# RWKV-7, gated delta rule, mLSTM and RG-LRU in one layer: another order of the groups, an output projection in three rounds, and a longer lag for the mixers' matmuls

## The chip, the cores and the metric

One core of one Trainium2 chip. The metric is the device time of one execution in microseconds; the kernel before took 1270.41 us (median of 3 runs, 1268.99 to 1271.3).

## The reference

One decoder layer on a sequence of 256 tokens with 2048 features, all in float32. The input is normalised and multiplied by one wide matrix; its columns feed four recurrent mixers of 512 features each. Their outputs side by side are multiplied by `w_out` and added to the input. A SwiGLU feed-forward part (hidden size 5632) and a last norm follow.

```python
n = rmsnorm(x, attn_norm[l])
u = n @ w_in[l]
u_gdn, u_mlstm, u_rglru, u_rwkv = jnp.split(u, MIXER_SPLITS, axis=-1)
y_gdn = gated_deltanet(u_gdn, ...)    # conv, l2norm, chunked delta rule with a triangular solve
y_mlstm = mlstm(u_mlstm, ...)         # conv, gates, running maximum, chunkwise attention form
y_rglru = rglru_block(u_rglru, ...)   # conv, two small matmuls, gates, linear scan, gelu gate
y_rwkv = rwkv7_time_mix(u_rwkv, ...)  # token shift, small matmuls, scan over chunks, norm, gate
mix = jnp.concatenate([y_gdn, y_mlstm, y_rglru, y_rwkv], axis=-1)
x = x + mix @ w_out[l]
n = rmsnorm(x, ffn_norm[l])
x = x + (jax.nn.silu(n @ ffn_w_gate[l]) * (n @ ffn_w_up[l])) @ ffn_w_down[l]
```

## The kernel before

Every large matrix product is made of three float32r matmuls (`mm3`, L167): both operands are split into a high and a low half, and high x high, high x low and low x high are summed. Weights come as units of 128 x 1024 values. `weights` (L149) loads one unit through SP's queue into one of four `raw` buffers; ScalarE then makes the high half (`whi`) and VectorE the low half (`wlo`), four buffers of each.

The input projection works in groups of 256 columns (`group`, L374). A group is four units with 24 matmuls of 256 columns each, summed in one PSUM bank of the tag `big`. An eviction follows (`shift_mix`, `conv`, `silu2`, `gelu2`), mostly on VectorE and ScalarE.

The mixers are Python generators, two halves of each mixer (`rwkv_half`, `gdn_half`, `mlstm_half`, `rglru_half`), with `gates_mm` and two `joint_solve` besides. `spawn` puts a generator on a list. After each unit `tick(0.65)` adds 0.65 to a counter, and for each whole number every generator on the list runs to its next `yield`, so that a piece of each mixer is written down between two units of the projection; `HOLD` lets a generator pass some ticks. The order in which instructions are written down is their priority, and for each engine the instructions are put into its queue by priority as soon as what they need has been queued. `high_priority(offset=n)` moves instructions n places earlier; weights are moved 20 places ahead (`PRIO`), evictions 40 (`EPRIO`). The mixers' matmuls and transposes go through `Lag` (L401), which places them `LAG` instructions later:

```python
def matmul(self, *a, **k):
    with self.em.tc.high_priority(offset=-LAG):
        return self.em.nc.tensor.matmul(*a, **k)
```

Their results go to four PSUM banks `mx` and one `mxl`. Scratch tiles in SBUF come from lists of slots (`SLOTS`: classes A, B and L of 512 values per partition, class D of 1024) that are handed out first in, first out.

The groups come in the order RWKV, RG-LRU, delta rule, mLSTM. `w_out` (L1183) multiplies the mixers' outputs by the output matrix: a run (L1195) is one quarter (512 columns) of the output and some of the eight mixer halves. Each half in it is one unit of 12 matmuls of 512 columns; a run ends with two additions from PSUM (L1213). Before the first use of a half, `run` ticks until the mixer has finished it and splits it (`split`, L1175). There are two rounds of four runs: first RWKV, RG-LRU and delta rule, then mLSTM. While generators are alive or the groups are under way, banks come from `big` alone (three); later from all eight in turn.

Of the kernel before, what the change touches and what calls it, by code (L numbers as in the profile page):

```python
# [14 lines left out]
D = 2048  # L15
# [6 lines left out]
OFF_GDN, OFF_ML, OFF_RG, OFF_RW = 0, 2056, 4112, 5136  # L22
CDEC = math.exp(-0.5)
TICKS = 0.65
LAG = 20
UNIT = 1024
PRIO = 20
EPRIO = 40
WARM = 14
TAIL = 3  # L30
HOLD = {("rw1", 17): 1, ("gates", 1): 1, ("rg0", 0): 1, ("rg1", 1): 3}
SLOTS = dict(A=12, B=11, L=4, D=16)
NRAW, NHI = 4, 4


RW, RG, GD, ML = OFF_RW, OFF_RG, OFF_GDN, OFF_ML
# [756 lines left out]
def gates_mm(em):  # L793
    nc = em.nc
    gs = em.S()
    ghi, glo = (gs.bitcast(F32R)[:, i * 256 : i * 256 + 256].rearrange("p (k n) -> p k n", k=KT) for i in range(2))
    nc.scalar.activation(ghi, em.gw, AF.Copy)
    nc.vector.tensor_tensor(glo, em.gw, ghi.bitcast(F32), op=ALU.subtract)
    z = em.mx()
    o = z[0:16, 0:T]  # L800
    for k in range(KT):
        em.mm3(o, ghi[:, k, :], glo[:, k, :], em.nhi[:, k, :], em.nlo[:, k, :], start=k == 0, stop=k == KT - 1)
    em.free(gs)
    g = em.S(2)
    gp = em.gp
    U, V = g[0:16, 0:T], g[0:16, T : 2 * T]
    N, B = g[0:16, 2 * T : 3 * T], g[0:16, 3 * T : 4 * T]
    nc.scalar.activation(U, o, AF.Identity, bias=gp[:, 0:1])
    nc.scalar.activation(gp[:, 1:2], gp[:, 1:2], AF.Exp)
    nc.scalar.activation(B, U, AF.Tanh, scale=0.5)  # L810
    nc.vector.tensor_scalar(B, B, 0.5, 0.5, op0=ALU.mult, op1=ALU.add)
    nc.scalar.activation(N, U, AF.Abs)
    nc.scalar.activation(N, N, AF.Exp, scale=-1.0)
    nc.vector.tensor_scalar(V, U, gp[:, 2:3], 0.0, op0=ALU.mult, op1=ALU.max)
    yield
    nc.scalar.activation(N, N, AF.Ln, bias=em.c_one[0:16])
    nc.vector.tensor_tensor(V, V, N, op=ALU.add)
    nc.vector.tensor_scalar(V, V, gp[:, 1:2], None, op0=ALU.mult)
    nc.vector.tensor_tensor_scan(N, em.rs16, V, 0.0, op0=ALU.mult, op1=ALU.add)
    em.free(em.gw_)  # L820
    em.ncd = em.dp.tile([4, T], F32, name="ncd", tag="ncd")
    nc.sync.dma_start(em.ncd, N[0:4, :])
    t = em.mx()
    for i, r in enumerate((U, N, B)):
        for a in range(2):
            em.pe.transpose(t[:, (i * 2 + a) * 16 : (i * 2 + a) * 16 + 16], r[:, a * P : a * P + P], em.ident[0:16, 0:16])
    GT = em.const([P, 3, 2, 16], "GT")
    nc.vector.tensor_copy(GT.rearrange("p i a n -> p (i a n)"), t[:, 0:96])
    em.free(g)
    em.ncs = GT[:, 1]  # L830
    em.nbeta = em.const([P, 2, 4], "nbeta")
    nc.vector.tensor_scalar(em.nbeta, GT[:, 2, :, 4:8], -1.0, None, op0=ALU.mult)
    em.beta = GT[:, 2, :, 4:8]
    em.neg = em.const([P, 4], "neg")
    nc.scalar.activation(em.neg, GT[:, 1, 1, 0:4], AF.Exp, scale=-1.0)
    nc.vector.tensor_scalar(em.neg, em.neg, -1.0, None, op0=ALU.mult)
    yield

    em.c = em.const([P, 2, 4], "ccol")
    nc.vector.tensor_tensor(em.c, GT[:, 0, :, 8:12], GT[:, 1, :, 12:16], op=ALU.add)  # L840
    t = em.mx()
    for a in range(2):
        em.pe.transpose(t[0:4, a * P : a * P + P], em.c[:, a, :], em.ident)
    M = em.S()
    nc.vector.tensor_copy(M[0:4, T : 2 * T], t[0:4, 0:T])
    nc.vector.tensor_tensor_scan(M[0:4, 0:T], M[0:4, T : 2 * T], M[0:4, T : 2 * T], 0.0, op0=ALU.max, op1=ALU.max)
    em.Md = em.dp.tile([4, T], F32, name="Md", tag="Md")
    nc.sync.dma_start(em.Md, M[0:4, 0:T])
    t = em.mx()
    for a in range(2):  # L850
        em.pe.transpose(t[:, a * 4 : a * 4 + 4], M[0:4, a * P : a * P + P], em.ident[0:4, 0:4])
    em.free(M)
    em.M = em.const([P, 2, 4], "Mcol")
    nc.vector.tensor_copy(em.M.rearrange("p a n -> p (a n)"), t[:, 0:8])
    em.enm = em.const([P, 2, 4], "enm")
    nc.vector.tensor_tensor(em.enm, GT[:, 1, :, 12:16], em.M, op=ALU.subtract)
    nc.vector.tensor_scalar(em.enm, em.enm, 80.0, None, op0=ALU.min)
    nc.scalar.activation(em.enm, em.enm, AF.Exp)
    em.mix["gates"] = 1
# [9 lines left out]
def gdn_half(em, hf, Q, K, V, SZ):  # L869
    nc = em.nc  # L870
    KQ = em.S(2)
    KQv = KQ.rearrange("p (s n) -> p s n", s=2)
    for s, X, bias in ((1, Q, em.c_lnq), (0, K, 0.0)):
        silu2(em, X)
        sq = em.S()
        nc.scalar.activation(sq, X, AF.Square)
        z = yield from sums(em, em.onesr, sq)
        rsqrt_ln(em, sq, z, em.c_4eps, ebias=bias)
        nc.vector.tensor_tensor(KQv[:, s, :], X, sq, op=ALU.mult)
        em.free(sq, X)  # L880
        yield
    silu2(em, V)
    z = em.mx()
# [25 lines left out]
    for g in range(2):  # L909
        z = em.mx()  # L910
# [8 lines left out]
    z = em.mx()  # L919
# [9 lines left out]
    for b in range(4):  # L929
        r = slice(32 * b, 32 * b + 32)  # L930
# [7 lines left out]
    X, XT = em.S(c="B"), em.S(c="B")  # L938
# [104 lines left out]
def mlstm_half(em, hf, Q, K, V1, SO, v1s):  # L1043
# [3 lines left out]
    while "gates" not in em.mix:  # L1047
        yield
    zb = bcast_rows(em, em.Md, hf)
    yield  # L1050
    Hs = em.S(c="B")
    ss = em.const([P, 2, 2], em.nm("mss"))
    rs = em.const([P, 2, 2], em.nm("mrs"))
# [126 lines left out]
    return hi, lo  # L1180


def w_out(em):  # L1183
    nc, A = em.nc, em.A
    xin = A["x"].rearrange("(a p) d -> p a d", p=P)
    em.x = {}
    for n in range(2):
        for a in range(2):
            em.x[a, n] = em.S(2)
            nc.sync.dma_start(em.x[a, n], xin[:, a, n * 1024 : n * 1024 + 1024])  # L1190
    em.xq = {(a, q): em.x[a, q // 2][:, (q % 2) * 512 : (q % 2) * 512 + 512] for a in range(2) for q in range(4)}
    row = {"gd": 0, "ml": 4, "rg": 8, "rw": 12}
    sp = {}

    def run(q, parts):  # L1195
        banks = [em.bank(), em.bank()]
        for i, (m, hf) in enumerate(parts):
            if (m, hf) not in sp:
                while (m, hf) not in em.mix:
                    em.tick()  # L1200
                sp[m, hf] = split(em, em.mix[m, hf])
                em.free(em.mix[m, hf])
            hi, lo = (t.bitcast(F32R) for t in sp[m, hf])
            whi, wlo = em.weights("w_out", row[m] + 2 * hf, 2, q * 512, 512)
            for a in range(2):
                for kk in range(2):
                    ts = slice(kk * T + a * P, kk * T + a * P + P)
                    em.mm3(banks[a], hi[:, ts], lo[:, ts], whi[:, kk, :], wlo[:, kk, :], start=i == 0 and kk == 0, stop=i == len(parts) - 1 and kk == 1)
            em.tick(TICKS)
            if q == 3:  # L1210
                em.free(*sp[m, hf])
        for a in range(2):
            nc.vector.tensor_tensor(em.xq[a, q], em.xq[a, q], banks[a], op=ALU.add)  # L1213

    early = [(m, h) for m in ("rw", "rg", "gd") for h in range(2)]
    late = [("ml", 0), ("ml", 1)]
    for q in range(4):
        run(q, early)
    ss = em.const([P, 2, 4], "ss1")

    def norm(q):
        em.transpose_in(lambda a, k: em.xq[a, q][:, (k % 4) * P : (k % 4) * P + P], em.PT["ffn_norm"], range(4 * q, 4 * q + 4))
        for a in range(2):
            junk = em.S()
            nc.scalar.activation(junk, em.xq[a, q], AF.Square, accum_out=ss[:, a, q : q + 1])
            em.free(junk)

    for q in range(4):
        run(q, late)
        if q:  # L1230
            norm(q - 1)

    def last():
        norm(3)
        em.rs1 = em.rstd(ss, "rs1")

    return last
# [119 lines left out]
def hybrid(tc, A, out, dbg=None, parts=("rw", "gd", "ml", "rg", "tail", "ffn")):  # L1357
    nc = tc.nc
    with ExitStack() as ctx:
# [36 lines left out]
        if "rw" in parts:  # L1396
# [3 lines left out]
            K1 = shift_mix(em, grp(RW + 768), (6, 7))  # L1400
            V1 = shift_mix(em, grp(RW + 1280), (10, 11))
            em.spawn("rw1", rwkv_half(em, 1, LX, R1, K1, V1))
        if "rg" in parts:
            wax = em.S(2)
            nc.gpsimd.dma_start(wax, A["rglru"])
            em.wa, em.wx = (wax[:, i * 512 : i * 512 + 512].rearrange("p (n j) -> p n j", n=4) for i in range(2))
            for hf in range(2):
                X = conv(em, grp(RG + 256 * hf), em.PT["rglru_conv"], 4, (2 * hf, 2 * hf + 1), bias=em.PT["rglru_conv_b"])
                Gt = gelu2(em, grp(RG + 512 + 256 * hf))
                em.spawn(f"rg{hf}", rglru_half(em, hf, X, Gt, wax))  # L1410
        if "gd" in parts or "ml" in parts:
            em.spawn("gates", gates_mm(em))
            em.gnh = em.const([P, 1], "gnh")
# [10 lines left out]
        if "ml" in parts:  # L1424
            for hf in range(2):
# [8 lines left out]
                nc.vector.tensor_scalar(SO, SO, 0.5, 0.5, op0=ALU.mult, op1=ALU.add)  # L1434
                Q, K = (conv(em, grp(ML + 512 * i + 256 * hf), em.PT["mlstm_conv"], 8, (4 * i + 2 * hf, 4 * i + 2 * hf + 1)) for i in range(2))
                em.spawn(f"ml{hf}", mlstm_half(em, hf, Q, K, V1, SO, v1s))
        if dbg:
            while em.gens:
                em.tick()
            for k, t in em.mix.items():  # L1440
                if isinstance(k, tuple) and k in dbg:
                    nc.sync.dma_start(dbg[k], t)
# [21 lines left out]
```

## Time and profile before

| | us |
|---|---|
| median of 3 runs | 1270.41 |
| lowest and highest run | 1268.99, 1271.3 |
| the profiled execution, its own time | 1272.06 |
| its span, first to last instruction | 1270.3 |
| TensorE busy in the span | 1241.6 |
| VectorE busy | 781.4 |
| ScalarE busy | 639.7 |

The profiled execution is one run of its own; what is counted in its span is set against its own time of 1272.06 us, 1.65 us above the median. Busy time of TensorE is that of the matmuls, which are pipelined: it doesn't say how many of them are in a stretch, so the number of instructions is read beside it. In waits, the name ahead of the arrow is the instruction that waited, the one behind it what ended the wait. L409 and L413 are the two lines of `Lag`, L169 to L171 the three matmuls of `mm3`; the weight halves show under L274.

### The profile page before, as it was taken

To read this page: it belongs to the slowest core of one execution; us is meant where nothing else is said; L and a number is where in the kernel's file an instruction comes from. 1 tells how busy PE (TensorE), PEld (TensorE's weight loads), DVE (VectorE), ACT (ScalarE), POOL (GpSimd) and SP (SyncE) were. 2 spreads that over 40 slices of the span, in tenths; PEclk is the share of its full clock that TensorE was granted. 3 is DMA by queue.
4 is the path that set the end of the run, shared out by engine and by line. 5 is a ranking of instruction groups with operands and counts; after the bars stand their busy time and mean duration, and the time that the engine had idled before them with its cause. 6 is when DMAs were issued, how large, how long until landed. Compare 5 with 4: busy or idle time off the path is not lost.

```text
span 1270.3 us, 18343 instructions
## 1 busy us (share of the span) xinstructions
PE 1241.6 (98%) x7216; PEld 1074.4 (85%) x7216; DVE 781.4 (62%) x1087; ACT 639.7 (50%) x849; POOL 31.9 (3%) x65
## 2 busy tenths in 40 slices
PE   9999999999989999999999999999999999999997
PEld 8899999998988888888888888888888888878885
DVE  7876799666798775744454444445455455556554
ACT  7755784436644454644444444444444444445443
POOL 1100000000000100000000000000000000001000
PEclk9999999999999999999999999999999999999999
DMA  9554436344654356566666666666666666666663
GB/s 345 170 177 144 142 124 197 109 138 133 193 160 131 110 177 192 177 187 184 192 197 184 189 193 188 203 205 198 185 190 192 189 189 188 195 198 185 197 190 109
DMA packets 72198, 226.97 MB, mean 179 GB/s; under 512 B 15752, under 2 KB 16016, under 8 KB 72112
## 3 DMA queue, kind: packets, MB, share of 16 engines
q1 hardware_dynamic: 71504, 224.14, 57.2%
q0 software_dynamic: 464, 1.57, 0.5%
q8 instruction: 56, 0.92, 0.3%
q14 instruction: 30, 0.25, 0.1%
q10 hardware_dynamic: 144, 0.10, 0.0%
HBM read 222.49 MB, written 3.28 MB: 178 GB/s over the span
## 4 chain that ended last, share of the span: by engine, by line
PE 88%; DVE 6%; ACT 2%; DMA 1%; issue 1%; POOL 0%; DVEq 0%; POOLq 0%; SPq 0%; ACTq 0%
PE big L171 14%; PE big L170 14%; PE big L169 13%; PE mx L169 10%; PE mx L171 10%; PE mx L170 10%; PE mx L409 4%; PE mxl L171 3%; PE mxl L169 3%; PE mxl L170 3%; DVE wlo L274 2%; PE big L277 2%; DVE sD L499 1%; DVE sD L500 1%; PE mx L413 1%
## 5 line engine op out<-in xcount | busy, mean ns | idle before, releaser
L274 DVE TENSOR_TENSOR wlo<-raw,whi 128x1024 fp32r<-128x1024 f32 x396 | 485.6, 1227 | 376.8 <-ACT whi L274 375.8
L274 ACT ACTIVATE whi<-raw 128x1024 fp32r<-128x1024 f32 x396 | 418.2, 1057 | 447.4 <-PE big L171 271.7
L170 PE MATMUL big<-wlo,nhi 128*128 128x512 f32 (+1 forms) x464 | 162.2, 350 | 0.9 <-DVE wlo L274 0.9
L169 PE MATMUL big<-whi,nhi 128*128 128x512 f32 (+1 forms) x464 | 161.9, 349 | 0.1
L171 PE MATMUL big<-whi,nlo 128*128 128x512 f32 (+1 forms) x464 | 161.7, 349 | 0.0
L171 PE MATMUL big<-nhi,wlo 128*128 128x256 f32 x544 | 158.8, 292 | 3.0 <-DVE wlo L274 3.0
L170 PE MATMUL big<-nlo,whi 128*128 128x256 f32 x544 | 158.6, 292 | 0.0
L169 PE MATMUL big<-nhi,whi 128*128 128x256 f32 x544 | 157.8, 290 | 0.0
L169 PE MATMUL mx<-whi,nhi 128*128 128x512 f32 x352 | 138.0, 392 | 0.0
L171 PE MATMUL mx<-whi,nlo 128*128 128x512 f32 x352 | 137.0, 389 | 0.0
L170 PE MATMUL mx<-wlo,nhi 128*128 128x512 f32 x352 | 137.0, 389 | 0.0
L171 PEld LDWEIGHTS big<-nhi,wlo 128*128 128x128 f32 x544 | 106.0, 195 | 4.9 <-DVE wlo L274 3.2
L170 PEld LDWEIGHTS big<-nlo,whi 128*128 128x128 f32 x544 | 105.8, 194 | 1.9 <-issue 0.7
L169 PEld LDWEIGHTS big<-nhi,whi 128*128 128x128 f32 x544 | 105.9, 195 | 1.4 <-issue 0.3
L170 PEld LDWEIGHTS big<-wlo,nhi 128*128 128x128 f32 x464 | 89.0, 192 | 12.3 <-DVE wlo L274 1.5
L169 PEld LDWEIGHTS big<-whi,nhi 128*128 128x128 f32 x464 | 89.0, 192 | 11.1 <-ACT whi L274 0.3
L171 PEld LDWEIGHTS big<-whi,nlo 128*128 128x128 f32 x464 | 89.1, 192 | 10.9
L169 PE MATMUL mx<-whi,sA 128*128 128x512 f32 x212 | 82.9, 391 | 0.7 <-ACT sA L1178 0.7
L170 PE MATMUL mx<-wlo,sA 128*128 128x512 f32 x212 | 82.5, 389 | 0.0
L171 PE MATMUL mx<-whi,sA 128*128 128x512 f32 x208 | 80.9, 389 | 0.0
L171 PEld LDWEIGHTS mx<-whi,nlo 128*128 128x128 f32 x352 | 66.1, 188 | 13.8
L170 PEld LDWEIGHTS mx<-wlo,nhi 128*128 128x128 f32 x352 | 66.1, 188 | 13.3
(424 smaller groups left out, 1786.4 us busy)
## 6 DMA issues: line engine op xcount, KB each, us to landing
raw<-in_units SPq DMA_DIRECT2D x404, 512.0 KB, 3.6
sD<-in_x SPq DMA_DIRECT2D x8, 512.0 KB, 5.1
sD<-in_xT SPq DMA_DIRECT2D x4, 512.0 KB, 6.3
out_y<-sD SPq DMA_DIRECT2D x8, 256.0 KB, 3.0
sA<-in_final_norm POOLq DMA_DIRECT2D x4, 256.0 KB, 5.9
sD<-in_lora SPq DMA_DIRECT2D x1, 512.0 KB, 6.6
sD<-in_rglru POOLq DMA_DIRECT2D x1, 512.0 KB, 3.8
dr<-sD SPq DMA_DIRECT2D x2, 256.0 KB, 4.2
```

Source lines behind the costliest of these rows:

```text
L169: i = nc.tensor.matmul(out, ahi, bhi, start=start, stop=False, skip_group_check=True)
L170: nc.tensor.matmul(out, ahi, blo, start=False, stop=False, skip_group_check=True)
L171: self.last_mm = nc.tensor.matmul(out, alo, bhi, start=False, stop=stop, skip_group_check=True)
L274: i = fn(*a, **k)
L277: i = fn(*a, **k)
L409: return self.em.nc.tensor.matmul(*a, **k)
L413: return self.em.nc.tensor.transpose(*a, **k)
L499: nc.vector.tensor_tensor(tv, col, row, op=ALU.mult)
L500: nc.vector.tensor_tensor(inv[:, j + 1 : n, 0:b], inv[:, j + 1 : n, 0:b], tv, op=ALU.add)
```

## The change

`LAG` goes from 20 to 44. The groups come in the order RWKV, delta rule, mLSTM, RG-LRU: the block of RG-LRU moves behind that of mLSTM with nothing in it changed. `w_out` works in three rounds of four runs: RWKV; mLSTM and RG-LRU; delta rule. A half is split one part ahead of its use (`ready`). Three yields are added: in `gates_mm` after the DMA of the running maximum, in `gdn_half` between the split and the matmuls of `sums`, and in `mlstm_half` after `bcast_rows`. The slots are divided otherwise; `TICKS` and `HOLD` stay.

```diff
-LAG = 20
+LAG = 44
...
-SLOTS = dict(A=12, B=11, L=4, D=16)
+SLOTS = dict(A=10, B=9, L=4, D=18)
...
     em.Md = em.dp.tile([4, T], F32, name="Md", tag="Md")
     nc.sync.dma_start(em.Md, M[0:4, 0:T])
+    yield
...
-        z = yield from sums(em, em.onesr, sq)
+        z = yield from sums(em, em.onesr, sq, 1)
...
     zb = bcast_rows(em, em.Md, hf)
-    yield
+    for _ in range(2):
+        yield
...
+ROUNDS = ([("rw", 0), ("rw", 1)], [("ml", 0), ("ml", 1), ("rg", 0), ("rg", 1)], [("gd", 0), ("gd", 1)])
...
+    def ready(m, hf):
+        if (m, hf) not in sp:
+            while (m, hf) not in em.mix:
+                em.tick()
+            sp[m, hf] = split(em, em.mix[m, hf])
+            em.free(em.mix[m, hf])
+
+    def run(q, r):
+
+        parts = ROUNDS[r]
         banks = [em.bank(), em.bank()]
         for i, (m, hf) in enumerate(parts):
-            if (m, hf) not in sp:
-                while (m, hf) not in em.mix:
-                    em.tick()
-                sp[m, hf] = split(em, em.mix[m, hf])
-                em.free(em.mix[m, hf])
+            ready(m, hf)
+            if i + 1 < len(parts):
+                ready(*parts[i + 1])
+            elif q == 3 and r + 1 < len(ROUNDS):
+                ready(*ROUNDS[r + 1][0])
...
-    early = [(m, h) for m in ("rw", "rg", "gd") for h in range(2)]
-    late = [("ml", 0), ("ml", 1)]
-    for q in range(4):
-        run(q, early)
+    for r in range(2):
+        for q in range(4):
+            run(q, r)
...
     for q in range(4):
-        run(q, late)
+        run(q, 2)
...
-        if "rg" in parts:
-            wax = em.S(2)
...
         if "gd" in parts or "ml" in parts:
             em.spawn("gates", gates_mm(em))
...
+        if "rg" in parts:
+            wax = em.S(2)
...
+                em.spawn(f"rg{hf}", rglru_half(em, hf, X, Gt, wax))
```

## Rows read from the trace of the kernel before

**Rows 1.** The page: its head and part 1.

```profile
span 1270.3 us, 18343 instructions
...
PE 1241.6 (98%) x7216; PEld 1074.4 (85%) x7216; DVE 781.4 (62%) x1087; ACT 639.7 (50%) x849; POOL 31.9 (3%) x65
```

**Rows 2.** Windows of one core; us, then busy us (instructions) of each engine.

```profile
61.00:107.00 46.00, 44.93 (x341) 43.23 (x342) 34.10 (x48) 21.71 (x29) 0.00 (x0) 0.93 0.58 175
107.00:165.00 58.00, 58.00 (x453) 54.29 (x452) 43.49 (x72) 41.45 (x62) 1.48 (x2) 1.00 0.46 134
165.00:305.00 140.00, 138.15 (x1325) 128.34 (x1324) 107.81 (x218) 74.48 (x105) 1.69 (x4) 0.99 0.49 150
305.00:436.00 131.00, 119.31 (x979) 114.33 (x979) 104.01 (x209) 67.23 (x105) 4.96 (x8) 0.96 0.47 145
436.00:461.00 25.00, 25.00 (x120) 20.38 (x120) 20.09 (x41) 16.22 (x35) 2.81 (x3) 1.00 0.44 135
```

**Rows 3.** Windows: the FFN.

```profile
540.00:1140.00 600.00, 600.00 (x2693) 497.69 (x2692) 295.98 (x262) 268.20 (x286) 2.19 (x4) 1.00 0.63 192
```

**Rows 4.** Waits of TensorE, 61 to 461 us: us in total, times, longest.

```profile
PE big L171 <- DVE wlo L274: 3.0, 1, 3.0
PE mx L409 <- DVE sA L1065: 2.9, 2, 2.5
PE mx L409 <- DVE sA L774: 2.8, 1, 2.8
PE mx L409 <- DVE sB L422: 2.3, 1, 2.3
PE mx L413 <- DVE sA L846: 1.9, 1, 1.9
PE mx L409 <- DVE sB L996: 1.5, 1, 1.5
PE big L170 <- DVE wlo L274: 0.9, 1, 0.9
PE mx L409 <- ACT sB L421: 0.8, 1, 0.8
```

**Rows 5.** Windows of 10 us at the four later drops of the clock.

```profile
195.00:205.00 10.00, 8.16 (x55) 8.14 (x56) 8.28 (x23) 3.02 (x6) 0.00 (x0) 0.83 0.60 184
318.00:328.00 10.00, 8.84 (x55) 8.20 (x55) 6.83 (x12) 9.62 (x11) 0.58 (x2) 0.83 0.42 133
390.00:400.00 10.00, 8.54 (x58) 8.54 (x59) 9.30 (x23) 3.36 (x8) 0.15 (x1) 0.83 0.37 107
431.00:441.00 10.00, 9.15 (x46) 7.92 (x46) 7.70 (x22) 5.79 (x16) 2.35 (x3) 0.83 0.28 80
```

**Rows 6.** Timeline, 371.5 to 376.5 us: start, us, engine, line.

```profile
375.10 0.69 DVE L774 SCALAR_TENSOR_TENSOR sA<-sA,sA 128x512 f32<-128x512 f32 x1
...
375.85 0.70 PE L409 MATMUL mx<-sA,sA 128*128 128x256 f32 x2 [2.85 <-DVE sA L774]
```

**Rows 7.** Windows: 256-column matmuls alone, and 512-column ones alone.

```profile
200.00:220.00 20.00, 20.00 (x166) 20.00 (x166) 17.96 (x41) 11.12 (x15) 0.00 (x0) 0.99 0.66 191
...
480.00:500.00 20.00, 20.00 (x90) 16.56 (x89) 10.74 (x11) 8.61 (x9) 0.00 (x0) 1.00 0.64 192
```

**Rows 8.** Waits of VectorE, 61 to 436 us.

```profile
DVE wlo L274 <- ACT whi L274: 31.3, 30, 3.3
DVE sB L696 <- PE mx L409: 6.2, 6, 2.2
...
DVE sA L985 <- PE mx L409: 0.2, 1, 0.2
```

**Rows 9.** Timelines of ScalarE and VectorE: the RG-LRU chain of one half.

```profile
171.34 1.28 ACT L1133 ACT_TABLE_LOAD   x1
...
188.87 0.67 DVE L1155 TENSOR_TENSOR sB<-sB,sA 128x512 f32<-128x512 f32 x1
```

**Rows 10.** Source line 1213, the addition that ends a run of w_out.

```profile
L1213 DVE TENSOR_TENSOR sD<-sD,big x9: 678/680/689, 454.7 to 530.5; 128x512 f32<-128x512 f32 x9
```

More of the change, by code (lines that the diff above doesn't have):

```diff
@@ L1193, in w_out @@
     sp = {}
-    def run(q, parts):
+    def ready(m, hf):
[6 more added lines that the diff above has]
+        parts = ROUNDS[r]
         banks = [em.bank(), em.bank()]
         for i, (m, hf) in enumerate(parts):
-            if (m, hf) not in sp:
-                while (m, hf) not in em.mix:
-                    em.tick()
-                sp[m, hf] = split(em, em.mix[m, hf])
-                em.free(em.mix[m, hf])
+            ready(m, hf)
[3 more added lines that the diff above has]
+                ready(*ROUNDS[r + 1][0])
             hi, lo = (t.bitcast(F32R) for t in sp[m, hf])
@@ L1402, in hybrid @@
             em.spawn("rw1", rwkv_half(em, 1, LX, R1, K1, V1))
-        if "rg" in parts:
-            wax = em.S(2)
[L1405 to L1410, printed above, removed]
         if "gd" in parts or "ml" in parts:
@@ L1436, in hybrid @@
                 em.spawn(f"ml{hf}", mlstm_half(em, hf, Q, K, V1, SO, v1s))
+        if "rg" in parts:
+            wax = em.S(2)
+            nc.gpsimd.dma_start(wax, A["rglru"])
+            em.wa, em.wx = (wax[:, i * 512 : i * 512 + 512].rearrange("p (n j) -> p n j", n=4) for i in range(2))
+            for hf in range(2):
+                X = conv(em, grp(RG + 256 * hf), em.PT["rglru_conv"], 4, (2 * hf, 2 * hf + 1), bias=em.PT["rglru_conv_b"])
+                Gt = gelu2(em, grp(RG + 512 + 256 * hf))
+                em.spawn(f"rg{hf}", rglru_half(em, hf, X, Gt, wax))
         if dbg:
```

## Prediction

> **What bounds the kernel now.** I read the page first. TensorE is busy for 1241.6 of 1270.3 us [rows 1], so a gain must come out of the 28.7 us in which it stands, or out of time in which its clock is low; no other engine is over 62%. Then I split the span. In the feed-forward part TensorE has no gap at all: 600.00 of 600 us [rows 3]. The change touches nothing there, so I leave it alone. The gaps lie between 61 and 436 us, where the input projection's matmuls alternate with those of the mixers [rows 2]: 1.07 + 0 + 1.85 + 11.69 = 14.6 us. The four stretches are those of the RWKV, RG-LRU, delta-rule and mLSTM groups, read off the weights that the matmuls take.
>
> Third, the list of waits [rows 4]. The first row (3.0 us) is a weight half at the very start of the stretch, before any mixer runs; the change doesn't reach it. The other seven sum to 2.9 + 2.8 + 2.3 + 1.9 + 1.5 + 0.9 + 0.8 = 13.1 us. In six of them a mixer's matmul stands first in TensorE's queue and its input is not there; in the seventh (0.9) the weight half is late behind the same burst on VectorE. The reader should see one such place close up [rows 6]: the matmul starts 0.06 us after the VectorE instruction that it needed ends, and TensorE idled 2.85 us, with weight tiles ready behind it.
>
> Fourth, the clock. After four of the waits the granted clock drops to its lower level (1.2 instead of 2.4 GHz): the mean over 10 us is 0.83 each time [rows 5], which is 0.17 x 10 = 1.7 us lost, 6.8 us in all. The low clock at 61 us (0.07 x 46 = 3.2 us [rows 2]) follows the wait that stays.
>
> So 13.1 + 6.8 = 19.9 us is what the change can reach. The rest of the 375 us I count as fixed work.
>
> **Part by part.**
>
> *The lag.* A mixer's matmul is queued 44 instead of 20 instructions behind its place in the program: 24 more. A unit of the input projection is 27 instructions (one DMA, two halves, 24 matmuls), so 24 instructions hold 24 x 24/27 = 21 matmuls. With 166 of them in 20 us, 0.120 us each [rows 7], TensorE has 2.56 us more of other work before it comes to ask for the input. That work exists: four pairs of weight halves are buffered, 4 x 24 x 0.120 = 11.5 us. All six waits on mixers were at most 2.85 us, so five go and 0.3 us stays. Only matmuls and transposes move. Their evictions follow them, and the small DMAs on SP follow the evictions, past at most one weight load; four raw buffers cover that, and without them one late weight half costs what the one in rows 4 does, 0.9 us. Removed: 13.1 - 0.3 = **12.8 us**, and with the four waits that are followed by a low clock **6.8 us**.
>
> *The added yields.* The transposes behind the mLSTM maximum scan (L846, 1.9 us), the first matmuls of the delta rule's norms (L422, 2.3 us) and the mLSTM's first scores get one more tick, 1/0.65 = 1.54 units = 4.4 us. They are a second cure for waits already counted, so they add nothing. Their price is a later finish: two ticks (8.9 us) for a delta half, one for an mLSTM half. The next part hides it.
>
> *The order of groups.* The delta rule's groups come four groups = 16 x 24 x 0.120 = 46 us earlier before the output projection, and they are now used last. Before, its tail ran in the last microseconds before the output projection begins at 436 us [rows 2], with no projection matmul left beside it: the wait on L996 and the low clock at 431 us [rows 4, 5]. With mLSTM, RG-LRU and two rounds (24 units) after it, that tail has cover. Counted above. Without cover it would cost the same 1.5 + 1.7 us again.
>
> *VectorE gets denser.* In 107 to 436 us it is busy 43.5 + 107.8 + 104.0 = 255.3 of 329 us, 78% [rows 2]. Delta and mLSTM tails that ran after 436 us now come before it. In 436 to 461 us VectorE did 20.1 us, about half of it weight halves, so I add 10 us and take off 2 for the RG-LRU half that goes the other way: 263 of some 310 us, 85%. Where it is full, waits can come back. Lower bound 0; upper bound the three waits of before in stretches where VectorE had no room (1.9, 2.8, 2.5 us, two of them with a low clock): 7.2 + 3.4 = 10.6 us. I take one of them with its clock, 2.5 + 1.7 = **4.2 us**, since the lag covers the others.
>
> *Three rounds.* Twelve runs of w_out instead of eight: four more runs, so eight more additions of 0.68 us on VectorE [rows 10], 5.4 us. A run has at least two units of 12 matmuls of 0.222 us [rows 7], 5.3 us, for two additions, 1.4 us. The rows of 480 to 500 us are such short runs, with TensorE busy throughout. But while mixers are alive there are only three banks to rotate, not eight. Bounds 0 and 5.4; I take **0.5 us**.
>
> *RG-LRU last.* Its second half is spawned with the last group and held for three ticks, so its first step comes after 7 units of w_out, and 44 instructions are two to three units there: it runs 24 to 27 us into w_out. Its chain took from 171.34 to 189.54, 18.2 us [rows 9]. It is wanted at unit 12, 29.3 us in: 13 to 16 us late. Against that stand 8.0 us of other units in the three free weight buffers, a chain that was timed with VectorE nearly full, and banks for the next runs. Bounds 0 and 8 + 1.7; nearer to 0, since both engines are half idle there: I take **2 us**.
>
> *The slots.* 59 slots of 512 before and after; a reader that holds one longer could delay a split. No row shows that; I take 0.
>
> Sum: -12.8 - 6.8 + 4.2 + 0.5 + 2.0 = -12.9 us. The profiled execution took 1272.06 us, so 1259.2 us; it stood 1.65 us above the median of the runs, so **1257.5 us**.
>
> **The rivals.** About 0.2%, 2.5 us, is what a measurement of this kernel can tell from no change: faster is below 1267.9 us, slower above 1272.9.
>
> *A. VectorE is the late one.* The three waits in its full stretches stay or grow, because the lag hides a late input once, not a queue that falls behind steadily. For it: VectorE's density. Against it: in 200 to 220 us it was busy 17.96 of 20 us and TensorE lost nothing [rows 7]. Time: -19.6 + 10.6 + 2.5 = -6.5, **1263.9 us**, and up to 1270 if the waits nearly double.
>
> *B. No new cost at all:* -19.6 us, **1250.8 us**.
>
> *C. Slower: evictions hold up VectorE's queue.* A matmul that comes 2.56 us later lets its eviction wait, and everything behind it on VectorE too. Before, VectorE stood 25.4 us in 28 waits for mixers' matmuls (13 rows, first and last in rows 8). If each grew by 2.56 us it would be 71.7 us more: 289.4 + 25.4 + 71.7 = 386.5 us for a stretch that lasted 375, so +11.5 us, **1281.9 us**. It turns slower from 60/28 = 2.15 us a wait. Against it: the waits already average 0.9 us behind 20 instructions, so the evictions seem to be queued after their matmul's new place, not its old one.
>
> The Trainium skill speaks for C (PSUM — Partial Sum Buffer, "Engine vs sequencer instructions"): VectorE's queue is strictly first in, first out, and matmuls start in program order. By that rule alone the later matmul is paid on VectorE too, and the time is C's. The rows agree as far as TensorE goes [rows 6].
>
> *D. Slower: RG-LRU uncovered.* If no other unit can run while its second half is awaited, w_out stands for the chain: 18.2 + 1.7 = 19.9 instead of the 2 taken, **1275.4 us**. It turns slower from 17.4 us. Against it: the free weight buffers.
>
> *E. The lag does nothing,* because matmuls already go when their inputs come. Then yields and order alone take 1.9 + 2.3 + 0.9 + 1.5 and three low clocks, 11.7 us, less 2.5: **1261.2 us**.
>
> **How the numbers follow.** Forecast 0.50, A 0.20, B 0.10, C 0.09, D 0.05, E 0.06. A splits 0.13 faster, 0.07 same. Faster 0.50 + 0.13 + 0.10 + 0.06 = 0.79, same 0.07, slower 0.14. The range runs from 1249 us (B less the 1.4 us by which the lowest run lies under the median, rounded down) to 1270 us (A's far end). It leaves out C and D, 0.14, and a little of B.
>
> **What would show it.** In the changed profile, TensorE's waits on L846, L422, L774, L1065 and L996 should be gone or under 0.5 us; the granted clock should drop once in the mixers' part (at 61 us), perhaps twice; TensorE's instruction count should not move. VectorE's idle time before L696 should stay near 6.2 us [rows 8]; if it doubles, C is at work. The addition of w_out should appear 24 times instead of 16. A wait of a w_out matmul on a split of RG-LRU is D. The forecast is wrong if new waits of several us stand on weight halves or on evictions in the delta-rule or mLSTM stretch, each with its own low clock behind it.

## The result, and the profile after

The changed kernel takes 1279.16 us (median of 4 executions, 1278.59 to 1281.58), the kernel before beside it 1270.86 us: a ratio of 1.0067, 95% interval 1.0054 to 1.0081. It is slower by 0.67%, 8.3 us; the prediction had it faster, and its range ended at 1270 us. The profiled execution took 1281.58 us; the spans of the two profiled executions differ by 9.5 us.

The page of the changed kernel, head and part 1, answers [rows 1]; TensorE does the same 7216 matmuls.

```profile
span 1279.8 us, 18372 instructions
...
PE 1242.9 (97%) x7216; PEld 1076.5 (84%) x7216; DVE 785.8 (61%) x1095; ACT 638.2 (50%) x848; POOL 31.6 (2%) x65
```

The start times of a few matmuls in the two traces show where the 9.5 us of span lie (us from the start of the span):

| | 1152 of the 2448 256-column matmuls done | first matmul of w_out | first of the feed-forward part | last matmul | end |
|---|---|---|---|---|---|
| before | 206.5 | 436.5 | 531.0 | 1260.8 | 1270.3 |
| after | 198.2 | 444.9 | 536.9 | 1266.8 | 1279.8 |
| after less before (unrounded times) | -8.3 | +8.5 | +6.0 | +5.9 | +9.5 |

The change is 8.3 us ahead when nearly half of the projection is done, and 8.5 us behind when w_out begins. w_out (384 matmuls of 512 columns) gives back 2.5 us, the feed-forward part nothing, and the tail, the time from the start of the last matmul to the end, is 13.1 instead of 9.5 us.

The same windows of both kernels, columns as in [rows 2] (the last three: granted clock, DMA share, GB/s). First the kernel before, then the changed one.

```profile
61.00:186.00 125.00, 123.93 (x962) 117.00 (x962) 97.66 (x165) 82.61 (x119) 2.43 (x3) 0.97 0.48 144
186.00:311.00 125.00, 123.15 (x1202) 114.69 (x1201) 91.64 (x180) 60.31 (x86) 0.74 (x3) 0.99 0.50 155
311.00:361.00 50.00, 46.37 (x354) 44.52 (x353) 39.31 (x72) 33.85 (x44) 1.05 (x2) 0.97 0.51 161
361.00:525.00 164.00, 155.94 (x996) 137.63 (x995) 120.62 (x217) 75.71 (x133) 7.41 (x10) 0.98 0.52 156
```

```profile
61.00:186.00 125.00, 123.88 (x992) 118.62 (x993) 95.59 (x164) 74.98 (x107) 2.54 (x4) 0.98 0.52 158
186.00:311.00 125.00, 120.76 (x1134) 111.08 (x1133) 85.11 (x173) 57.93 (x81) 1.92 (x4) 0.93 0.46 140
311.00:361.00 50.00, 38.35 (x280) 37.66 (x279) 47.11 (x97) 22.14 (x35) 2.33 (x4) 0.86 0.44 134
361.00:525.00 164.00, 161.60 (x1078) 143.76 (x1076) 120.95 (x201) 92.71 (x151) 4.99 (x7) 1.00 0.53 162
```

Over the four windows TensorE stands 19.4 instead of 14.6 us. From 361 us on the changed kernel is better: TensorE stands 2.40 instead of 8.06 us and its clock doesn't drop up to 525 us. Two windows ahead of that are worse. In 186 to 311 us it stands 4.24 instead of 1.85 us at a clock of 0.93; in 311 to 361 us it stands 11.65 instead of 3.63 us at 0.86, and VectorE is busy 47.11 of 50 us. The clock is low for 17.1 + 10.2 + 3.4 = 30.7 us of these two windows, where before it was low for 6.8; counted by half that is 15.4 us lost instead of 3.4.

TensorE's waits from 61 to 470 us, as in [rows 4]:

```profile
PE big L170 <- DVE wlo L274: 8.2, 1, 8.2
PE mx L409 <- DVE sB L1067: 3.4, 1, 3.4
PE big L171 <- DVE wlo L274: 3.0, 1, 3.0
PE mx L409 <- DVE sB L670: 2.4, 2, 1.6
PE mx L409 <- DVE sB L916: 1.6, 1, 1.6
PE mx L409 <- DMA sB<-dr: 1.0, 1, 1.0
PE mx L409 <- DVE sB L422: 0.7, 1, 0.7
```

The waits on L846, L774 and L421 are gone, that on L996 (now L997) is down from 1.5 us to pieces of at most 0.3, and L422 is down from 2.3 to 0.7. L1067 (the old L1065) is not, and a weight half is late by 8.2 us.

**One sum over whole executions.** Span times mean clock is the span with every microsecond at the low clock counted by half. For the profiled executions it is 1270.3 x 0.990 = 1257.6 before and 1279.8 x 0.982 = 1256.8 after; over all executions the medians are 1257.2 (70 of the kernel before) and 1256.9 (4). By this count the two kernels are level but for the clock. The count hides two things. It counts by half the low clock of the tail too (4.8 us before, 7.8 after), where TensorE has no matmuls. And the tail is 3.6 us longer, which is no loss of clock: with the 8.6 us that the low clock ahead of the tail costs more (37.5 us instead of 20.4, by half), the two come to 12.2 us, so 2.7 of them were saved elsewhere.

**Place 1, 225 to 245 us.** The window of the changed kernel; before, TensorE was busy for 20.00 us of it at a clock of 1.00.

```profile
225.00:245.00 20.00, 17.64 (x216) 15.81 (x216) 6.89 (x10) 4.82 (x5) 0.00 (x0) 0.73 0.47 145
```

SP's issues in the changed kernel show a possible reason: the raw weight loads stop.

```profile
192.89 13.23 SPq L274 DMA_DIRECT2D raw<-in_units  x5
212.97 2.53 SPq L932 DMA_DIRECT2D dr<-sB  x4
215.69 0.35 SPq L274 DMA_DIRECT2D raw<-in_units  x1
...
227.65 17.10 SPq L274 DMA_DIRECT2D raw<-in_units  x6
```

L932 is a block DMA of the delta rule, now in this stretch because its groups come second instead of third. It waits 7.2 us at the head of SP's queue for VectorE's L916. Behind it stand the raw loads; then come the twelve DMAs that read the RWKV solve back, so only one raw load is issued between 206 and 227.65 us. In TensorE's order the small RWKV matmuls after the read-back stand alone from 231.6 to 239.9 us. The clock is low from 234.4 for 17.1 us.

**Place 2, 311 to 331 us.** VectorE's timeline:

```profile
319.51 0.29 DVE L500 TENSOR_TENSOR sD<-sD,sD 32x135 f32<-32x135 f32 x1
319.83 0.69 DVE L741 TENSOR_TENSOR sA<-sA,sB 128x512 f32<-128x512 f32 x1
320.56 0.31 DVE L499 TENSOR_TENSOR sD<-sD,sD 32x156 f32<-32x156 f32 x1
...
329.41 0.38 DVE L499 TENSOR_TENSOR sD<-sD,sD 32x220 f32<-32x220 f32 x1
329.82 1.22 DVE L274 TENSOR_TENSOR wlo<-raw,whi 128x1024 fp32r<-128x1024 f32 x1
```

The delta rule's block solve (L499, L500), the end of both RWKV halves (L741 to L745) and convolution steps (L763) fill VectorE without a gap from 311.6 us, and no weight half is among them until 329.82; the one ahead of it began at 310.41. ScalarE had made three high halves by 322.07 us, so what was late is VectorE:

```profile
319.13 2.94 ACT L274 ACTIVATE whi<-raw 128x1024 fp32r<-128x1024 f32 x3
```

TensorE waits 8.2 us for the low half, and the clock is low for 10.2 us from 326.5. Before, the solve began at 350.3 us, 30 us after the last L745 had ended.

**The tail.** ScalarE, the last work of the feed-forward part and the first square of the final norm:

```profile
1256.65 1.04 ACT L274 ACTIVATE whi<-raw 128x1024 fp32r<-128x1024 f32 x1
1267.04 0.63 ACT L274 ACTIVATE sA<-sD 128x512 f32<-128x512 f32 x1 [9.35 <-PE big L170]
```

The square's scratch tile takes a slot of class A (now 10 instead of 12) that the last splits' matmuls still read: ScalarE stands 9.35 us until they are over. Before, that square ran 4.9 us before the last matmul started.

### The profile page after: what moved, and what is told of

It is laid out like the page before. It is cut to its first block, busy times and chain, and to the rows that moved or that the text cites. A ratio compares the mean times of both kernels' runs of the same rounds, so it can differ in the third digit from the quotient of the medians.

```text
span 1279.8 us, 18372 instructions
## 1 busy us (share of the span) xinstructions
PE 1242.9 (97%) x7216; PEld 1076.5 (84%) x7216; DVE 785.8 (61%) x1095; ACT 638.2 (50%) x848; POOL 31.6 (2%) x65
## 4 chain that ended last, share of the span: by engine, by line
PE 85%; DVE 8%; DMA 3%; ACT 2%; issue 1%; POOL 0%; SPq 0%; DVEq 0%; POOLq 0%; ACTq 0%
PE big L171 13%; PE big L169 13%; PE big L170 13%; PE mx L171 10%; PE mx L170 10%; PE mx L169 10%; PE mx L409 4%; PE mxl L171 3%; PE mxl L170 3%; PE mxl L169 3%; DVE wlo L274 2%; PE big L277 2%; DVE sD L499 1%; DMA raw<-in_units 1%; DVE sD L500 1%
## 5 line engine op out<-in xcount | busy, mean ns | idle before, releaser
L274 ACT ACTIVATE whi<-raw 128x1024 fp32r<-128x1024 f32 x396 | 417.9, 1057 | 437.1 <-PE big L171 282.4
L170 PE MATMUL big<-wlo,nhi 128*128 128x512 f32 (+1 forms) x448 | 156.4, 349 | 8.2 <-DVE wlo L274 8.2
L169 PE MATMUL big<-whi,nhi 128*128 128x512 f32 (+1 forms) x448 | 157.0, 350 | 0.0
L171 PE MATMUL big<-whi,nlo 128*128 128x512 f32 (+1 forms) x448 | 156.6, 350 | 0.0
L169 PE MATMUL mx<-whi,sA 128*128 128x512 f32 x216 | 84.4, 391 | 0.2 <-ACT sA L1180 0.2
L171 PE MATMUL mx<-whi,sA 128*128 128x512 f32 x216 | 84.2, 390 | 0.2 <-DVE sA L1181 0.2
L169 PE MATMUL big<-whi,sA 128*128 128x512 f32 x208 | 81.2, 391 | 0.0
L171 PE MATMUL big<-whi,sA 128*128 128x512 f32 x208 | 80.9, 390 | 0.1
```

Source lines behind the costliest of these rows:

```text
L169: i = nc.tensor.matmul(out, ahi, bhi, start=start, stop=False, skip_group_check=True)
L170: nc.tensor.matmul(out, ahi, blo, start=False, stop=False, skip_group_check=True)
L171: self.last_mm = nc.tensor.matmul(out, alo, bhi, start=False, stop=stop, skip_group_check=True)
L274: i = fn(*a, **k)
```

## The experiments

All ratios are to the kernel before, run beside each. "Clock" is the median of the executions' mean granted clock, "weighted" the median of span times clock; "w_out" the start of its first matmul, "tail" the time from the start of the last matmul to the end, both of the profiled execution.

| run | median us | ratio, 95% interval | clock | weighted | w_out | tail |
|---|---|---|---|---|---|---|
| before | 1271.49 | | 0.990 | 1257.2 | 436.5 | 9.5 |
| after | 1279.16 | 1.0067 [1.0054, 1.0081] | 0.984 | 1256.9 | 444.9 | 13.1 |
| e1_lag20 | 1282.51 | 1.0093 [1.0064, 1.0121] | 0.982 | 1257.8 | 449.9 | 13.1 |
| e2_lag44_old | 1275.11 | 1.0032 [1.0022, 1.0043] | 0.991 | 1261.5 | 440.3 | 9.5 |
| e3_old_order | 1279.36 | 1.0069 [1.0048, 1.0089] | 0.990 | 1264.8 | 417.3 | 13.1 |
| e4_pool_dma | 1283.40 | 1.0097 [1.0077, 1.0116] | 0.986 | 1263.6 | 445.3 | 13.1 |
| e5_new_slots_old | 1276.99 | 1.0065 [1.0035, 1.0095] | 0.990 | 1261.6 | 434.4 | 13.1 |
| e6_delta_late | 1281.26 | 1.0078 [1.0060, 1.0096] | 0.985 | 1260.0 | 441.0 | 13.1 |
| e7_blocks_late | 1282.40 | 1.0077 [1.0053, 1.0102] | 0.983 | 1257.2 | 445.6 | 13.1 |
| e8_all_three | 1273.71 | 1.0033 [1.0013, 1.0052] | 0.987 | 1254.2 | 440.5 | 9.5 |
| e9_blocks_pool | 1280.52 | 1.0070 [1.0049, 1.0091] | 0.984 | 1257.4 | 437.7 | 13.2 |
| e10_all_four | 1271.78 | 1.0005 [0.9991, 1.0018] | 0.988 | 1254.2 | 438.0 | 9.6 |
| e11_old_order_rounds | 1266.17 | 0.9959 [0.9943, 0.9975] | 0.993 | 1255.6 | 416.7 | 9.5 |
| e12_best_lag20 | 1266.70 | 0.9963 [0.9950, 0.9975] | 0.993 | 1255.4 | 421.9 | 9.5 |
| e13_rounds_only | 1272.46 | 1.0011 [1.0001, 1.0020] | 0.990 | 1257.3 | 437.1 | 9.4 |
| e14_blocks_pool_again | 1279.95 | one execution | 0.982 | 1255.2 | 443.3 | 13.2 |
| e16_yields_only | 1274.78 | 1.0026 [1.0015, 1.0037] | 0.989 | 1258.1 | 421.3 | 9.5 |

**The lag.** e1 is the changed kernel, e2 the kernel before, each with the other's lag:

```
-LAG = 44        # e1, in the changed kernel
+LAG = 20
-LAG = 20        # e2, in the kernel before
+LAG = 44
```

> The changed kernel with the lag back at 20. Theory S (the order of the groups: the delta rule's small transfers and the RWKV read-back now follow each other on SP's queue, and the delta solve falls on the RWKV tail on VectorE): both stalls stay, 1274 to 1282 us. Theory L (the lag: matmuls queued later make their evictions late, and these hold up the queues behind them): the stalls go, 1258 to 1266 us.

> The kernel before with the lag at 44 and nothing else changed. Theory S: the six waits on mixers' matmuls shrink as forecast, 1255 to 1266 us. Theory L: new waits behind late evictions, 1275 us or more.

In e1 the loss stays: the lag is not to blame. In e2 the time rises by 3.5 us, and TensorE stands 18.8 us between 61 and 525 us, 4.2 more than before. Two of the waits that the lag was to remove are longer, and in place of those on L846 and L996 stand waits of 1.9 and 1.7 us on L819 and L985. TensorE's waits of e2, 61 to 461 us:

```profile
PE mx L409 <- DVE sA L1065: 3.7, 1, 3.7
PE big L169 <- ACT whi L274: 3.3, 2, 3.1
PE mx L409 <- DVE sA L774: 3.3, 1, 3.3
PE big L171 <- DVE wlo L274: 3.3, 1, 3.3
PE mx L413 <- DVE sD L819: 1.9, 1, 1.9
```

L774 has 3.3 us instead of 2.8, L1065 3.7 in one instead of 2.5 [rows 4]. The matmul behind L774 has 2160 projection matmuls ahead of it instead of 2155: 5 more, not 21. The one behind L1065 does have 22 more (2263 for 2241), but it starts at 396.0 instead of 391.5 us. The two inputs came 1.9 and 4.6 us later, more than 5 and 22 matmuls of 0.120 us take (0.6 and 2.6 us). These inputs hang on earlier matmuls which are placed later as well; this last is an argument, no run took it apart.

**The order of the groups.** e3 puts RG-LRU back in second place and leaves the rest as changed; e11 also puts mLSTM into the last round and takes the squares' scratch from class B:

```
-    V1 ...; spawn rw1; gd groups; ml groups; rg groups      # e3, e11
+    V1 ...; spawn rw1; rg groups; gd groups; ml groups
-ROUNDS = (rw, ml + rg, gd)                                  # e11
+ROUNDS = (rw, rg + gd, ml)
-        junk = em.S()                                       # e11, in square()
+        junk = em.S(c="B")
```

> The changed kernel with the RG-LRU groups back in second place; lag, yields, rounds and slots as changed. Theory S: both stalls go, 1254 to 1266 us. Theory L: they stay in some form, 1274 us or more.

> The changed kernel with RG-LRU back in second place, the three rounds as RWKV, then RG-LRU with the delta rule, then mLSTM, and the squares' scratch from class B: what differs from the kernel before is the lag, the yields, the slot counts and a first round of its own for RWKV. Theory S (the old order has neither of the two crowded places, and only the wrong mixer in round 2 took the gain of 19 us back): the first w_out matmul near 417, w_out's first 480 matmuls take 95 to 100 us instead of 117, tail 9.5, the time 1255 to 1260. Rival G: the mixers' work left over at 417 us has to be done in w_out, which takes 110 us or more, and the time is 1268 to 1273.

With the old order place 1 has no low stretch and place 2 one of 3.4 us; w_out starts at 417 us, 28 us before the changed kernel's. e3 pays it back: its round 2 asks for mLSTM, which that order finishes last, and from its first matmul to the first of the feed-forward part w_out takes 116.8 us, where the kernel before took 94.5 (the expectation of e11 calls this stretch 480 matmuls; w_out has 384). e11 takes 108.5 us for it and is faster than both kernels, by 0.4% against the kernel before; it was expected at 1255 to 1260. Its windows, 186 us on:

```profile
186.00:311.00 125.00, 124.61 (x1214) 115.74 (x1215) 91.56 (x175) 62.84 (x86) 2.68 (x6) 1.00 0.54 163
311.00:361.00 50.00, 46.85 (x365) 45.70 (x364) 38.01 (x64) 37.59 (x51) 0.00 (x0) 0.97 0.53 160
361.00:525.00 164.00, 156.01 (x987) 135.21 (x986) 129.71 (x241) 76.89 (x139) 7.51 (x9) 0.98 0.53 156
```

Its gain has four possible carriers besides the scratch tile: the lag, the rounds, the yields and the slot counts (alone in e5, below). e12 takes the lag out of it again, e13 adds the three rounds alone to the kernel before, e16 the added yields alone:

```
-LAG = 44                                                    # e12, in e11
+LAG = 20
-    early, late = [rw, rg, gd], [ml]                        # e13, in the kernel before
+ROUNDS = (rw, rg + gd, ml)
+    yield                        # e16, in the kernel before: behind the DMA of Md,
-        z = yield from sums(em, em.onesr, sq)               # in the delta rule's norms,
+        z = yield from sums(em, em.onesr, sq, 1)
+    for _ in range(2):           # and at the start of an mLSTM half (one yield before)
+        yield
```

> The 1266-us kernel (old order, three rounds with mLSTM last, scratch from class B) with the lag back at 20. Theory W (the lag is worth what the forecast gave it where no crowd hides it): the waits on VectorE's tiles come back, 1276 to 1279. Theory R (the rounds carry the gain, the lag nothing): within 3 us of 1266.

> The kernel before with nothing but w_out in three rounds: RWKV, then RG-LRU with the delta rule, then mLSTM. Theory R (a first round that needs RWKV alone lets w_out start some 20 us earlier and fills the last waits of the groups): first w_out matmul near 417 instead of 436.5, time 1266 to 1268. Theory W or the yields: the start moves but the waits stay, 1270 to 1273.

> The kernel before with nothing but the added yields: one after the DMA of the mLSTM running maxima, one in the delta rule's sums, one more in the mLSTM half. The forecast and theory R: no effect, 1271.4 within 1 us. Rival: later tracing of the mixers' steps moves a wait, more than 2 us either way.

The lag is worth nothing here either. The rounds alone leave w_out's start at 437.1 us and the time within 0.2%. The yields alone start w_out at 421.3 us, but its first 96 matmuls take 43.2 us instead of 25.3 and the kernel is 0.26% slower. So e11's gain belongs to the parts together; which of them make it stays open. e16 shows one thing more, in its list of TensorE's waits from 61 to 470 us:

```profile
PE mx L409 <- DVE sA L1067: 4.1, 1, 4.1
PE big L171 <- DVE wlo L274: 3.2, 1, 3.2
PE mx L413 <- ACT sA L1090: 2.5, 1, 2.5
PE mx L409 <- DVE sB L422: 1.4, 1, 1.4
```

There is no wait on L846 or L774 in that list, with the old order and the lag at 20. All four kernels of the old order with the yields (e3, e11, e12, e16) have neither; the four without them (before, e2, e5, e13) wait 2.6 to 3.6 us for L774. Those with the yields have a wait for L1090 instead, of 2.5 us in e16 and 5.7 to 6.6 in the other three.

**Place 2 and the block DMAs.** e6 and e7 are to hold back the delta rule's solve and its half:

```
+    while key == "gd" and ("rw", 1) not in em.mix:          # e6, joint_solve
+        yield
+    while "rwS" not in em.mix:                              # e7, gdn_half, before L932
+        yield
+    for _ in range(3):
+        yield
```

> The changed kernel with the delta rule's block solve held back until both RWKV halves are done. Theory S (VectorE has the solve and the RWKV tail of both halves at once, and the lo of the next weights comes late): the 8.2-us wait for wlo near 322 us is gone, the low clock there is at most 3.4 us instead of 10.2, the place gives 6 us back, the time is about 1273. Rival G (what one stall gives back the next takes, since the mixers' chains set the end of the groups): the wait goes or moves, the first w_out matmul stays within 2 us of 444.9 and the time within 2 us of 1279.

> The changed kernel with the delta rule's four block DMAs per half issued only after the RWKV solve has been read back, so that SP does not stand for 7.2 us at the first of them in front of the raw loads. Theory S (that row of SP starves the projection near 229 us): the raw loads of 204 to 228 us go out without the gap, the low stretch of 17.1 us falls to 3.4 or goes, the place gives 8 us back, the time is about 1271. Rival G: the first w_out matmul stays within 2 us of 444.9 and the time within 2 us of 1279.

e6 did not do what its label says: the second solve starts at 311.7 us, 2.8 us earlier than in the changed kernel, and still runs among the RWKV lines. The 8.2-us wait on wlo is gone, but 5.5 us on whi stand in the same place; w_out starts 3.9 us earlier, yet the time does not fall. Nor did e7: the four DMAs stayed at 212 us in SP's queue, and place 1 is unchanged, so it says nothing on SP's part in it. What it did move is place 2: 305 to 331 us of e7 has TensorE busy 23.70 us at a clock of 1.00, where the changed kernel had 17.86 at 0.91. The solve (from 315.04 us) and the RWKV tail meet there too, but two weight halves stand among them, and TensorE waits 2.7 us in place of 8.2:

```profile
315.04 0.18 DVE L499 TENSOR_TENSOR sD<-sD,sD 32x31 f32<-32x31 f32 x1
...
323.45 1.22 DVE L274 TENSOR_TENSOR wlo<-raw,whi 128x1024 fp32r<-128x1024 f32 x1
...
326.17 0.69 DVE L745 TENSOR_TENSOR sA<-sA,sB 128x512 f32<-128x512 f32 x1
...
329.12 1.23 DVE L274 TENSOR_TENSOR wlo<-raw,whi 128x1024 fp32r<-128x1024 f32 x1
```

So the meeting of the two pieces is not enough; what differs is that the changed kernel has 18 us between two weight halves there, and e7 at most 9. e7's gain there is lost further on, with a low stretch of 10.2 us at 390.5.

**Place 1.** e4 puts all the small solve DMAs on POOL's queue, e9 and e14, the same kernel profiled a second time, the delta rule's block DMAs alone:

```
-    nc.sync.dma_start(dr[4 * b : ...], u4(MT)[r, :, r])     # L932, and L933
+    nc.gpsimd.dma_start(dr[4 * b : ...], u4(MT)[r, :, r])   # e4: L512, L513, L660, L661, L945, L946 too
```

> The changed kernel with the small transfers of the solves (both mixers' read-back, the delta rule's blocks) issued from POOL instead of SP, so that no weight load stands behind them. Theory S: the stall at 225 to 245 us and the low clock behind it go, the one at 322 to 331 us stays: 1264 to 1271 us. Theory L: nothing changes, 1277 to 1281 us.

> The changed kernel with only the delta rule's five block DMAs per half (four to the scratch tensor, one back) on POOL's queue; the RWKV read-back stays on SP. Holding the block DMAs back by a few steps left them at the same place of SP's queue, so this moves them off it. With it TensorE's order has projection matmuls among the RWKV ones after the read-back, as the kernel before has. Theory S (SP standing at the first block DMA keeps the raw loads back, and the RWKV matmuls then run alone at the low clock): raw loads go out between 206 and 217 us, the 17.1-us low stretch is at most 3.4 us, 7 us come back, the first w_out matmul near 438 and the time about 1272. Rival G (what one stall gives back the next takes): the low stretch shrinks, but the time stays within 2 us of 1279.

> The kernel with the block DMAs on POOL's queue once more, for a second profiled execution. Theory S (the row of RWKV matmuls alone made the 17.1-us low stretch): none of more than 3.4 us between 225 and 260 us; if this execution is one of the longer ones, at a clock of 0.982 to 0.984, its low stretches lie at other places, near 317 and 351 us. If instead a stretch of 10 us or more is back near 234 us with projection matmuls standing among the RWKV ones, S's account of that place falls.

In e4 the low stretch falls to 3.4 us, but the read-back is late: waits of 5.6 and 4.3 us on DMAs, and the weighted span rises by 6.7 us. In e9 five raw loads run on to 214.6 us where they had stopped at 206.1, and the RWKV matmuls have projection matmuls among them. Its profiled execution has no low stretch there, takes 1274.4 us, and looks like a full cure; its other five, on the same chip, take 1279 to 1282 us. e14 profiled one of that length, on another chip. The two executions of this one kernel, e9 first:

```profile
225.00:235.00 10.00, 10.00 (x152) 9.47 (x151) 1.22 (x3) 3.77 (x4) 0.00 (x0) 1.00 0.72 225
235.00:250.00 15.00, 14.41 (x170) 12.16 (x170) 10.98 (x21) 6.85 (x10) 0.00 (x0) 1.00 0.30 86
```

```profile
225.00:235.00 10.00, 10.00 (x153) 9.51 (x151) 1.52 (x2) 3.71 (x4) 0.00 (x0) 1.00 0.72 228
235.00:250.00 15.00, 14.61 (x120) 12.12 (x115) 8.04 (x16) 1.52 (x3) 0.00 (x0) 0.56 0.22 72
```

TensorE does the same instructions in the same order in both, and from 70 to 235 us they are 0.07 to 0.24 us apart. Then one stays at 2.4 GHz and the other spends 13.7 us at 1.2 GHz and falls 5.4 us further behind. One thing did differ earlier: the first low stretch, 3.4 us long in both, began at 60.6 us in e9 and at 62.6 in e14. So the clock at place 1 falls or stays with SP's raw loads on time and with projection matmuls among the small ones; the row of small matmuls standing alone is not what decides it, and that account falls. The order bears on how often it happens: of the 9 profiled executions with the changed order 8 have a low stretch that begins between 231 and 242 us (3.4 to 17.1 us long); of the 8 with the old order none has one that begins between 200 and 310 us. But a profile is one execution: four of the ten executions of e5, which has the old order, took 1285 to 1287 us at a clock of 0.981 to 0.982, and none of these was profiled.

**The slots.** e5 gives the kernel before the new slot counts; e8 joins e6, e7 and the scratch tile of class B, e10 adds e9's edit:

```
-SLOTS = dict(A=12, B=11, L=4, D=16)                         # e5, in the kernel before
+SLOTS = dict(A=10, B=9, L=4, D=18)
-        junk = em.S()                                       # e8, e10, in square()
+        junk = em.S(c="B")
```

> The kernel before with nothing but the changed kernel's slot counts (A 10, B 9, D 18 for A 12, B 11, D 16). Theory T (the smaller class A makes the first square of the end wait for the last feed-forward split's readers): the time from the last matmul's start to the end of the span goes from 9.5 to 13.0 us, the rest stays, the time is about 1274.4. Rival (the longer tail comes from the order of the groups or the rounds): the tail stays 9.5 and the time 1271, within 1 us.

> The changed kernel with the solve held back, the block DMAs late, and the scratch tile of the end's squares taken from class B. Theory S with T: the three add up, 6 + 8 + 3.5 us, tail 9.5, the time about 1262. Rival G with T: only the tail's 3.5 us comes back, 1275.5. Both wrong: the tail stays 13.0.

> The changed kernel with the block DMAs on POOL's queue, the delta rule's half and solve held back, and the squares' scratch from class B. Theory S with T: the 1273.7 of the three edits together less the 7 us of the low stretch near 232 us, about 1266.5. Rival G: within 2 us of 1273.7.

e5 has the tail of 13.1 us with the old order, and every kernel with the scratch from class B has 9.5 or 9.6. The whole of e5's loss is 5.2 us by the medians, and its executions spread from 1273.7 to 1286.9 us; the tail explains 3.6 of it. That square in e8 (ScalarE's timeline):

```profile
1252.36 1.04 ACT L274 ACTIVATE whi<-raw 128x1024 fp32r<-128x1024 f32 x1
1257.53 0.63 ACT L274 ACTIVATE sB<-sD 128x512 f32<-128x512 f32 x1 [4.13 <-DVE sD L274]
```

It now waits 4.13 us for the addition, not 9.35 us for the matmuls. e8 gives 5.5 us of the 17.5 expected, 3.6 of them in the tail; place 1 keeps its 17.1 us of low clock. e10 is level with the kernel before, not better.

## Why the prediction was wrong

- **The lag (-12.8 us of waits): the step that failed first.** I held the inputs fixed and moved the matmuls by 21 others. e2 shows 5 and 22, inputs that come 1.9 and 4.6 us later, and TensorE standing 4.2 us more instead of 12.8 less; e1 and e12 show no gain from the lag in either order. Rival E named this ("the lag does nothing") but kept the gain of the rest.
- **The waits that went.** Five of the six waits on mixers did go or shrink, and from 361 to 525 us TensorE stands 5.7 us less. With the lag back at 20 the same large waits are absent too, so it wasn't the lag; on L846 and L774 e16 shows that the yields alone remove them. That the delta rule's tail "has cover" fits the wait on L996 and the low clock at 431 us, both gone; no run took it apart from the rest. New waits more than made up for it: 19.4 us in all for 14.6.
- **VectorE gets denser (+4.2, at most 10.6): mis-sized.** I took the mean over 310 us. At 311 to 330 us the solve and the RWKV tail meet with no weight half among them, and that one place shows 8.2 us of wait and 10.2 us at half speed, 5.1 us: 13.3 us, over my upper bound. This is rival A's mechanism, beyond the 1270 us that I gave it. e7 has both pieces there with weight halves among them, 2.7 us of wait and no low clock. What the place costs in the end isn't shown, since e7 is no faster.
- **Low clock (-6.8 us): wrong sign.** The old drops went, but new ones came of 17.1, 10.2 and 3.4 us. I priced a drop at 1.7 us because the clock was low for 3.4 us at all four of before. Ahead of the tail the profiled executions have 20.4 us of low clock before and 37.5 after, 8.6 us of loss more.
- **SP ("past at most one weight load", covered): the mechanism was missed.** SP stood 7.2 us. What that cost isn't settled: e9 takes it away and its median stays.
- **The slots (0): wrong.** +3.6 us in the tail, shown by e5 and e8.
- **The yields (0): mis-sized.** As a cure for L846 and L774 they worked without the lag, but alone they cost 0.26%, 3.2 us (e16), where the prediction had their price hidden.
- **Three rounds (+0.5) and RG-LRU last (+2): about right.** L1227 runs 24 times; e13 is within 0.2%; no matmul of w_out waits for an RG-LRU split, and w_out takes 92.0 instead of 94.5 us.
- **Rival C was not it,** though the time came out near its 1281.9. VectorE's waits for mixers' matmuls grew from 25.4 to 33.1 us, not by 71.7, and 6.9 of that is one wait at place 1. At place 2 a weight half came behind the mixers' work on VectorE though its high half was there; with the lag at 20 (e1) the wait is still 7.3 us, and with the old order (e3, e11) it is absent, so the order of the groups put that work there, not the lag. The Trainium skill (PSUM — Partial Sum Buffer, "Engine vs sequencer instructions") has VectorE's queue as strictly in order. The trace of place 2 agrees with that: 329.82 us for the low half, 322.07 for the last of the three high halves.

What stays open: what decides the clock at place 1, where 17.1 of the 37.5 us of low clock lie; and which parts of e11 make its 0.4%.

## What to carry to other kernels

Before a reordering, lay the long pieces of the second engine on the new order and see where they leave no room for the pieces that the first engine waits for; a mean load over the whole stretch hides it. Multiply span by mean clock first: if that is equal, look for what slowed the clock, and look at the tail by itself. A scratch tile's class has a last reader, and a smaller class can put it on the tail; and where times of one kernel spread, one profiled execution can show a cure that the median does not have.

## What was not expected of the hardware

Two executions of one kernel ran the same matmuls within 0.24 us of each other from 70 to 235 us, and then one was granted 2.4 GHz and the other 1.2 GHz for 13.7 us, at a price of 5.4 us. Over the 17 rows of the table the weighted span runs from 1254.2 to 1264.8 us. Of the changed kernel's 9.5 us, the low clock ahead of the tail accounts for 8.6, counted by half, and the tail for 3.6; about 2.7 us came back elsewhere.
